# Where the weight sums for the last down projection are made: from the first layer's feed-forward part to the second layer's mixer

## The chip, the cores and the metric

The kernel runs on one core of a Trainium2 chip. The metric is device time in microseconds, the median of several runs. The engines are called by their names in the profile: PE is TensorE, PEld its weight loads, DVE is VectorE, ACT is ScalarE, POOL is GpSimd and SP is SyncE, which here only issues transfers.

## What is computed

A trunk of two layers over 512 tokens of width 1024, in float32. Each layer has three parallel mixers (a state recurrence, a chunked retention, a gated spatial unit), whose outputs are projected, gated and added, then an output projection and a feed-forward part with a short convolution. A root-mean-square norm stands before each half and at the end. Cut to what matters:

```
for l in range(2):
    h = rmsnorm(x, norm1_g[l])
    p = h @ w_in[l]
    y_rw, y_ret, y_sg = recurrence(p), retention(p), gating(p)
    proj = einsum('bsgc,gcd->bsgd', stack([y_rw, y_ret, y_sg]), w_branch[l])
    x = x + sum(sigmoid(gates(p)) * proj) @ w_out[l]
    x = x + conv_ffn(rmsnorm(x, norm2_g[l]), ffn_w_up[l], conv_w[l], conv_b[l], ffn_w_down[l])
return rmsnorm(x, final_g)
```

## The kernel before

Matrix products run in a float32 form that rounds its operands, so every operand is split in two: `hi` is the rounded value (a cast on ACT, line 139 for weights), `lo` what is left (a subtraction on DVE, line 140). A product is then three matmuls (line 156). Weights come in units of 128 rows by 512: SP loads a unit into a buffer called `wr` (line 126), ACT and DVE split it into `wh`/`wl` or `sh`/`sl`, and PE uses it for 12 matmuls of 128 x 512 in most stages. The order of the units is known from a first pass of the program (`plan`). A number by stage (`AHEAD`, 3 in the merges) says how many units ahead of the use a unit is split; three buffers `wr` (`NRAW`) let SP load ahead of that.

Products collect in PSUM: four accumulators `acc` and four tiles `sm`. In SBUF lie shared pools of tiles of 128 x 512 float32: `u` (`NU`, 31 tiles), `r` (16) and, outside the recurrence, `f` (39).

A scheduler orders the instructions on each engine: program order is priority, and what is not ready by its model of time may be passed by what is. On the chip each engine and each queue then runs its list in order. `keep_in_program_order` (written `po`) lets an instruction go only after the instruction traced just before it on its engine; what is traced later may still go ahead of it.

A layer's mixer begins with the projection and preparation of the recurrence (`rwkv`, `solve`), then its eight chunks. In a chunk PE's small matmuls (line 664) alternate with a copy `xb` on DVE (line 687), a copy `U` on ACT (line 701) and the state update on DVE (lines 712 and 713). Between these links `fill` puts units of other projections (`fillers`: gates, retention, gating) on PE. For each pair of chunks the output is normed (lines 723 to 733), with a power on POOL (line 732). After the recurrence come the gating projection and the recurrence's output (`sgu_v`, `rwkv_out`), then a list of steps, `SEQ`: S, H, U and Y are retention and gating steps, and 0, 2 and 1 are merges of the three branches, eight of each. A merge is one unit on PE, the gate loaded back by POOL (line 1034) and a product with it on DVE (line 1037); the sum over branches is made on POOL for branch 2 and on DVE for branch 1 (line 1040). From the 18th step on, `SEQ` has only merges. `wout` is the output projection: eight results of two units each, the residual sum (line 1051), the norm's operands (line 215) and squares (line 222).

The last down projection of the second layer is done as a fast product of halves with seven instead of eight products. For it four combinations of each group of four 128 x 512 tiles of the weight `wdt` are needed. They don't depend on the input, but the kernel makes them: `presum` loads four tiles `pre` on POOL's queue (line 253), makes four additions and subtractions on DVE in place (lines 242 to 245) and stores the results to HBM on POOL's queue (line 248). There are 11 such groups. They are made in the first layer: four in the up projections, with 16 tiles of the pool `f`, seven in the down projection, with tiles of the pool `u`. `last` reads the results as units named `tsum` (`ts` in the profile).

Of the kernel before, what the change touches and what calls it, by code (L numbers as in the profile page):

```python
# [15 lines left out]
L = 2  # L16
# [6 lines left out]
NU, NR, NFP = 31, 16, 39  # L23
FILL = (36, 2, 1)
KEPT = 6
PRE = {(0, "f", 2): 0, (0, "f", 4): 1, (0, "f", 6): 2, (0, "f", 8): 3, (0, "d", 0): 4, (0, "d", 1): 5, (0, "d", 2): 6, (0, "d", 3): 7,
       (0, "d", 4): 8, (0, "d", 5): 9, (0, "d", 6): 10}
SEQ = "0 H 0 S 0 U S U S 0 S 0 0 S 2 2 Y 0 0 2 1 2 1 2 1 2 1 2 1 2 1 1 1"
NRAW = 3
AHEAD = {None: 2, "p": 4, "r": 3, "f": 3, "u": 5, "q": 4}  # L30
# [21 lines left out]
class Emit:  # L52
    def __init__(self, ctx, tc, a, plan=None):

        self.plan, self.used = plan, []
        self.raws, self.parts, self.nraw, self.npart = [], [], 0, 0
        self.pool, self.fp, self.pin, self.keep, self.turn = None, None, False, False, 4
        self.tc, self.nc, self.a = tc, tc.nc, a
        tp = lambda n, b, **k: ctx.enter_context(tc.tile_pool(name=n, bufs=b, **k))
        self.cp = tp("cp", 1)  # L60
        self.wp = tp("wp", 2)
        self.up = tp("up", NU)
        self.rg = tp("rg", NR)
# [57 lines left out]
    def load(self, u):  # L121
        name, l, i, c0, n, _ = u
        raw = self.u(n="wr") if u[5] == "q" and self.nraw % 2 else self.wp.tile([128, 512], F32, name=self.nm("wr"), tag="wr", bufs=NRAW)
        src = self.tsum[i] if name == "tsum" else self.a[name][l, i]
# [112 lines left out]
    def presum(self, l, stage, m):  # L237

        if self.pre:
            q, b = self.pre.pop()  # L240
            V = self.nc.vector
            V.tensor_tensor(b[3], b[3], b[1], op=SUB)
            V.tensor_tensor(b[1], b[1], b[0], op=SUB)
            V.tensor_tensor(b[0], b[0], b[3], op=ADD)
            V.tensor_tensor(b[2], b[2], b[0], op=SUB)
            for p, t in zip((7, 5, 6, 4), (b[3], b[1], b[0], b[2])):
                self.tsum[q, p] = self.dp.tile([128, 512], F32, name=self.nm("ts"))
                self.nc.gpsimd.dma_start(self.tsum[q, p], t)
        q = PRE.get((l, stage, m))
        if q is not None:  # L250
            b = self.fpre.pop(0) if stage == "f" else [self.u(n="pre") for _ in range(4)]
            for i, t in enumerate(b):
                self.nc.gpsimd.dma_start(t, self.a["wdt"][0, 2 * q + i // 2][:, i % 2 * 512:i % 2 * 512 + 512])
            self.pre.append((q, b))
# [69 lines left out]
    def run(self):  # L324
        nc, tc, a, V = self.nc, self.tc, self.a, self.nc.vector
        self.con = self.cp.tile([128, NCC], F32, name="con")
        self.pre, self.tsum = [], {}
# [52 lines left out]
    def mixer(self, l, nst):  # L380
        self.pool = None
        with self.tc.tile_pool(name=f"rw{l}", bufs=1) as rp:
            self.rwp = rp
            self.filler = self.fillers(l)
# [18 lines left out]
        for step in (sg, sg, out, sg, None, out, sg, out, out):  # L403
            next(step) if step else self.sgu_bias()
        yrw, ysg, mg, out, m2 = self.yrw, [], [], [], 0
# [3 lines left out]
        for step in SEQ.split():  # L409
# [51 lines left out]
    def rwkv(self, l, nst):  # L461
# [211 lines left out]
        for c in range(8):  # L673
# [13 lines left out]
            V.tensor_copy(xb, Q[:, 1])  # L687
            self.fill(FILL[2], True)
# [12 lines left out]
            A.copy(U, P1[:, 1])  # L701
            self.fill(FILL[2], True)
# [4 lines left out]
            if c < 7:  # L707
# [3 lines left out]
                else:  # L711
                    V.tensor_tensor(St, St, Q[:, 0], op=ADD)
                    po(V.tensor_tensor(St, St, f, op=MUL))
            py = P1[:, 0]
# [328 lines left out]
    def wout(self, l, mg, xd, st):  # L1043
        nc, V = self.nc, self.nc.vector
        out = []
        for m in range(8):
# [6 lines left out]
            self.norm_z(st, xi, "n2")  # L1053
            self.norm_sq(st, xi)
# [3 lines left out]
    def ffn_up(self, l, st, x):  # L1058
# [58 lines left out]
    def ffn_down(self, l, act, x, st):  # L1117
# [3 lines left out]
        for m in range(8):  # L1121
# [8 lines left out]
            self.presum(l, "d", m)  # L1130
# [3 lines left out]
    def last(self, act):  # L1134
# [8 lines left out]
        def unit(p, q):  # L1143
            if p > 3:
                return self.unit("tsum", 0, (q, p), 0)
# [290 lines left out]
```

## Time and profile before

| | us |
|---|---|
| median of 3 runs | 1705.17 (1704.99 to 1705.78) |
| the profiled execution's own time | 1701.58 |
| its span, first to last instruction | 1699.7 |
| PE busy | 1687.0 |
| PEld busy | 1379.7 |
| DVE busy | 1233.1 |
| ACT busy | 799.9 |
| POOL busy | 240.8 |

The granted clock is 0.999 over the span. A busy time counts an engine's instructions from start to end; matmuls are pipelined, so PE counts as busy even where a matmul starts a little later than it could. The chain of waits follows the last instruction back to what released it, step by step. A row of a group names the line, the engine, the operation, what it writes and reads, and the count. Times along the span are in microseconds from its start.

### The profile page before, as it was taken

The numbers are of one execution on the slowest core, as the hardware profiler recorded it, in microseconds if no ns is written. First come the engines' busy times: TensorE is split into PE (matmuls) and PEld (weight loads), VectorE is DVE, ScalarE is ACT, GpSimd is POOL, SyncE is SP. The second block draws the span as 40 slices with busy tenths as digits, with TensorE's granted clock in tenths as the row PEclk, the third lists the DMA queues.
The fourth block names the chain that finished last, engine by engine and source line by source line (L and its number), as shares of the span: only waits on it lengthen the run. The fifth ranks groups of instructions, "written<-read, shape, count | busy, mean of one in ns | idle before, by whom it ended". The sixth has DMA issues, their size and how long they took to land.

```text
span 1699.7 us, 27885 instructions
## 1 busy us (share of the span) xinstructions
PE 1687.0 (99%) x10214; PEld 1379.7 (81%) x10214; DVE 1233.1 (73%) x2157; ACT 799.9 (47%) x1367; POOL 240.8 (14%) x336
## 2 busy tenths in 40 slices
PE   9999999999999999999999999999999999999998
PEld 7888777888888888888888888777888888887786
DVE  6887746578669887655568888455775698888776
ACT  6563433554355444433355644335542554444565
POOL 2121000003301200003321210000132022110000
PEclk9999999999999999999999999999999999999999
DMA  5236552524544532147743365525254443433774
GB/s 182 87 108 203 177 179 94 181 92 161 189 146 147 194 123 95 63 145 260 255 142 100 97 211 172 180 94 188 85 173 149 155 136 132 130 131 112 241 243 167
DMA packets 147768, 260.01 MB, mean 153 GB/s; under 512 B 19600, under 2 KB 39952, under 8 KB 147632
## 3 DMA queue, kind: packets, MB, share of 16 engines
q1 hardware_dynamic: 122960, 192.87, 35.2%
q0 software_dynamic: 15888, 49.95, 8.7%
q10 hardware_dynamic: 8784, 15.42, 2.6%
q8 instruction: 80, 1.31, 0.3%
q14 instruction: 56, 0.46, 0.1%
HBM read 212.94 MB, written 45.22 MB: 152 GB/s over the span
## 4 chain that ended last, share of the span: by engine, by line
PE 90%; DVE 4%; DMA 3%; issue 1%; ACT 1%; SPq 0%; ACTq 0%; DVEq 0%
PE acc L156 82%; PE sm L156 3%; PE sm L664 2%; DVE wl L140 1%; DMA wr<-wall 1%; PE sm L917 1%; PE sm L571 1%; DMA tr<-bkT 1%; DVE sl L140 0%; PE sm L1022 0%; ACT wh L139 0%; DVE cs L790 0%; DMA wr<-ts 0%; DVE TMP L788 0%; DMA x<-xT 0%
## 5 line engine op out<-in xcount | busy, mean ns | idle before, releaser
L156 PE MATMUL acc<-lo,sh 128*128 128x512 f32 x1108 | 431.8, 390 | 0.5 <-ACT sh L139 0.5
L156 PE MATMUL acc<-hi,sh 128*128 128x512 f32 x1108 | 431.9, 390 | 0.0
L156 PE MATMUL acc<-hi,sl 128*128 128x512 f32 x1108 | 430.3, 390 | 0.2 <-DVE sl L140 0.2
L139 ACT CAST sh<-wr 128x512 fp32r<-128x512 f32 (+1 forms) x375 | 228.3, 615 | 370.3 <-PE acc L156 217.6
L140 DVE TENSOR_TENSOR sl<-wr,sh 128x512 fp32r<-128x512 f32 (+1 forms) x375 | 254.5, 684 | 103.5 <-ACT sh L139 78.3
L140 DVE TENSOR_TENSOR wl<-wr,wh 128x512 fp32r<-128x512 f32 x238 | 166.5, 703 | 144.5 <-ACT wh L139 141.1
L139 ACT CAST wh<-wr 128x512 fp32r<-128x512 f32 x238 | 146.8, 619 | 244.4 <-PE acc L156 160.3
L156 PEld LDWEIGHTS acc<-lo,sh 128*128 128x128 f32 x1108 | 208.0, 188 | 45.0 <-ACT sh L139 1.2
L156 PEld LDWEIGHTS acc<-hi,sl 128*128 128x128 f32 x1108 | 208.0, 188 | 44.1 <-DVE sl L140 0.7
L156 PEld LDWEIGHTS acc<-hi,sh 128*128 128x128 f32 x1108 | 208.0, 188 | 43.1 <-issue 0.3
L156 PE MATMUL acc<-lo,wh 128*128 128x512 f32 x588 | 232.3, 395 | 0.3 <-DVE lo L215 0.2
L156 PE MATMUL acc<-hi,wl 128*128 128x512 f32 x588 | 229.8, 391 | 0.5 <-DVE wl L140 0.5
L156 PE MATMUL acc<-hi,wh 128*128 128x512 f32 x588 | 229.3, 390 | 0.0
L156 PEld LDWEIGHTS acc<-lo,wh 128*128 128x128 f32 x588 | 110.5, 188 | 25.5 <-DVE lo L215 1.5
L156 PEld LDWEIGHTS acc<-hi,wl 128*128 128x128 f32 x588 | 110.4, 188 | 25.4 <-DVE wl L140 1.5
L156 PEld LDWEIGHTS acc<-hi,wh 128*128 128x128 f32 x588 | 110.6, 188 | 22.5 <-issue 0.2
L156 PE MATMUL acc<-ah,sh 128*128 128x512 f32 x352 | 108.4, 389 | 0.0
L1084 ACT ACTIVATE cv<-fu,pc 128x512 f32<-128x512 f32 x88 | 71.6, 816 | 61.1 <-DVE fu L1082 59.8
L1082 DVE TENSOR_TENSOR fu<-acc,rsF 128x512 f32<-128x512 f32 x88 | 60.6, 688 | 39.8 <-PE acc L156 39.7
L156 PE MATMUL acc<-wl,hi 128*128 128x512 f32 x212 | 86.1, 406 | 0.0
L156 PE MATMUL acc<-wh,lo 128*128 128x512 f32 x212 | 82.8, 391 | 0.0
L156 PE MATMUL acc<-wh,hi 128*128 128x512 f32 x212 | 82.7, 390 | 0.0
(359 smaller groups left out, 2426.8 us busy)
## 6 DMA issues: line engine op xcount, KB each, us to landing
wr<-wall SPq DMA_DIRECT2D x488, 256.0 KB, 2.8
gd<-gth ACTq DMA_DIRECT2D x48, 256.0 KB, 3.0
gth<-gd POOLq DMA_DIRECT2D x48, 256.0 KB, 3.5
pre<-wdt POOLq DMA_DIRECT2D x44, 256.0 KB, 5.9
ts<-pre POOLq DMA_DIRECT2D x44, 256.0 KB, 2.8
wr<-ts SPq DMA_DIRECT2D x44, 256.0 KB, 3.9
wr<-wdn SPq DMA_DIRECT2D x40, 256.0 KB, 4.2
wr<-wdt SPq DMA_DIRECT2D x33, 256.0 KB, 3.6
```

The source lines that it names most:

```text
L139: self.kept(self.nc.scalar.copy(hi[:, :n], raw[:, :n]))
L140: self.kept(self.nc.vector.tensor_tensor(lo[:, :n], raw[:, :n], hi[:, :n], op=SUB))
L156: i = self.nc.tensor.matmul(*x, **y, **kw)
L571: i = T.matmul(pK[hv[1 - h], j, :], bk[hv[h], c, 1, :], x[hv[h], c, :], start=True, stop=True)
L664: po(T.matmul(o, l, r, start=start, stop=True, skip_group_check=True))
L917: po(T.matmul(X[h][:, i, :], lhsT, rhs, start=new[h], stop=stop, skip_group_check=True))
L1082: V.tensor_tensor(u, ps, self.rsF, op=MUL)
L1084: A.activation(t, u, AF.Identity, scale=self.p("cw2", j), bias=self.p("cb", j))
```

## The change

The groups of four sums are made in the second layer instead. A generator `sums` does it in steps: four loads on POOL; an empty step; then each operation on DVE, followed one step later by its store on POOL; each is kept behind what was traced before it on its engine. `presum` advances the generator: three times in each chunk of the second recurrence (after the copy `xb`, after the copy `U`, after the state update), once for each of the nine steps after it, twice for each of the 16 late steps of `SEQ`, and in the output projection five times for the first result and twice for each other. In the first layer the generator is empty. Four tiles of an own pool `pp` hold the loads. The pool `u` grows from 31 to 33 tiles, and the area for the descriptors of POOL's transfers is set to 4096 bytes a partition; the 16 tiles of `f` and the tiles of `u` are no longer taken for the sums.

```diff
-NU, NR, NFP = 31, 16, 39
+NU, NR, NFP = 33, 16, 39
-PRE = {(0, "f", 2): 0, (0, "f", 4): 1, (0, "f", 6): 2, (0, "f", 8): 3, (0, "d", 0): 4, (0, "d", 1): 5, (0, "d", 2): 6, (0, "d", 3): 7,
-       (0, "d", 4): 8, (0, "d", 5): 9, (0, "d", 6): 10}
+RING = 4096
...
+        self.pp = tp("pp", 4)
...
-    def presum(self, l, stage, m):
-
-        if self.pre:
-            q, b = self.pre.pop()
-            V = self.nc.vector
-            V.tensor_tensor(b[3], b[3], b[1], op=SUB)
-            V.tensor_tensor(b[1], b[1], b[0], op=SUB)
-            V.tensor_tensor(b[0], b[0], b[3], op=ADD)
-            V.tensor_tensor(b[2], b[2], b[0], op=SUB)
-            for p, t in zip((7, 5, 6, 4), (b[3], b[1], b[0], b[2])):
-                self.tsum[q, p] = self.dp.tile([128, 512], F32, name=self.nm("ts"))
-                self.nc.gpsimd.dma_start(self.tsum[q, p], t)
-        q = PRE.get((l, stage, m))
-        if q is not None:
-            b = self.fpre.pop(0) if stage == "f" else [self.u(n="pre") for _ in range(4)]
+    def sums(self, l):
+
+        P, V, po = self.nc.gpsimd, self.nc.vector, self.tc.keep_in_program_order
+        for q in range(NFF // 2 if l else 0):
+            b = [self.pp.tile([128, 512], F32, name=self.nm("pre"), tag="pre") for _ in range(4)]
             for i, t in enumerate(b):
-                self.nc.gpsimd.dma_start(t, self.a["wdt"][0, 2 * q + i // 2][:, i % 2 * 512:i % 2 * 512 + 512])
-            self.pre.append((q, b))
+                po(P.dma_start(t, self.a["wdt"][l - 1, 2 * q + i // 2][:, i % 2 * 512:i % 2 * 512 + 512]))
+            yield
+            yield
+            for p, o, x, op in ((7, 3, 1, SUB), (5, 1, 0, SUB), (6, 0, 3, ADD), (4, 2, 0, SUB)):
+                po(V.tensor_tensor(b[o], b[o], b[x], op=op))
+                yield
+                self.tsum[l, q, p] = self.dp.tile([128, 512], F32, name=self.nm("ts"))
+                po(P.dma_start(self.tsum[l, q, p], b[o]))
+            yield
+
+    def presum(self, n=1):
+        for _ in range(n):
+            next(self.sum, None)
...
-            self.filler = self.fillers(l)
+            self.filler, self.sum = self.fillers(l), self.sums(l)
...
         for step in (sg, sg, out, sg, None, out, sg, out, out):
             next(step) if step else self.sgu_bias()
+            self.presum()
...
-        for step in SEQ.split():
+        for i, step in enumerate(SEQ.split()):
+            self.presum(2 if i > 16 else 0)
...
             V.tensor_copy(xb, Q[:, 1])
+            self.presum()
             self.fill(FILL[2], True)
...
             A.copy(U, P1[:, 1])
+            self.presum()
             self.fill(FILL[2], True)
...
                     po(V.tensor_tensor(St, St, f, op=MUL))
+            self.presum()
...
             self.norm_z(st, xi, "n2")
+            self.presum(2 if m else 5)
             self.norm_sq(st, xi)
...
-        if l == 0:
-            self.fpre = [[self.f(n="pre") for _ in range(4)] for _ in range(4)]
         for i in range(NFF):
-            if l == 0 and i % 2 == 0 and 2 <= i <= 10:
-                self.presum(l, "f", i)
...
             xd.append(d)
-            self.presum(l, "d", m)
...
-        nc = _bacc.Bacc("TRN2", target_bir_lowering=False, num_devices=1)
+        nc = _bacc.Bacc("TRN2", target_bir_lowering=False, num_devices=1, dynamic_dma_scratch_size=RING)
```

More of the change, by code (lines that the diff above doesn't have):

```diff
@@ L123, in load @@
         raw = self.u(n="wr") if u[5] == "q" and self.nraw % 2 else self.wp.tile([128, 512], F32, name=self.nm("wr"), tag="wr", bufs=NRAW)
-        src = self.tsum[i] if name == "tsum" else self.a[name][l, i]
+        src = self.tsum[(l, *i)] if name == "tsum" else self.a[name][l, i]
         with self.tc.high_priority():
@@ L326, in run @@
         self.con = self.cp.tile([128, NCC], F32, name="con")
-        self.pre, self.tsum = [], {}
+        self.tsum = {}
         self.rst = self.cp.tile([128, 512], F32, name="rst")
@@ L1144, in unit @@
             if p > 3:
-                return self.unit("tsum", 0, (q, p), 0)
+                return self.unit("tsum", L - 1, (q, p), 0)
             return self.unit("wdt", 0, 2 * q + (p > 1), 512 * (p == 3))
```

## The prediction

> **What bounds the kernel now.** I read the busy times first, then the chain of waits, then the busy times by stage, then the waits around the sums.
>
> ```profile
> span 1699.7 us, 27885 instructions
> PE 1687.0 (99%) x10214; PEld 1379.7 (81%) x10214; DVE 1233.1 (73%) x2157; ACT 799.9 (47%) x1367; POOL 240.8 (14%) x336
> PE 90%; DVE 4%; DMA 3%; issue 1%; ACT 1%; SPq 0%; ACTq 0%; DVEq 0%
> ```
>
> TensorE is busy for nearly the whole span and makes 90% of the chain that ended last. Whether it runs at its pace is read from the long pieces of the chain:
>
> ```profile
> 509.76 355.19 PE acc L156 x1567
> ...
> 1262.79 94.05 PE acc L156 x414
> ...
> 1357.30 210.36 PE acc L156 x928
> ```
>
> 355.19 / 1567 = 0.2267 us for each matmul, the same in the second layer (210.36 / 928 = 0.2267), and 0.2272 in the stretch of the second layer's merges and output projection. The granted clock is 1.00 in these stages (next table), so a unit of 12 such matmuls takes 2.72 us and no stage runs below it. Only matmuls that start late can be won or lost.
>
> The busy times by stage (columns: window, its length, PE, PEld, DVE, ACT and POOL busy with counts, granted clock, DMA share, GB/s). The rows are: the first layer's output projection and feed-forward part, the second layer's recurrence, its gating projection, its early merges, its late merges, its output projection, and the passage into the last product.
>
> ```profile
> 460.00:860.00 400.00, 400.00 (x1766) 331.34 (x1765) 285.25 (x449) 170.11 (x274) 49.38 (x92) 1.00 0.48 161
> 1060.00:1142.00 82.00, 81.78 (x1180) 63.32 (x1178) 42.22 (x86) 30.46 (x59) 7.15 (x7) 1.00 0.44 141
> 1142.00:1208.00 66.00, 65.29 (x319) 53.25 (x315) 39.30 (x73) 35.27 (x64) 3.58 (x4) 1.00 0.45 144
> 1208.00:1265.00 57.00, 57.00 (x342) 47.58 (x341) 46.30 (x95) 26.23 (x51) 15.23 (x19) 1.00 0.44 148
> 1265.00:1309.00 44.00, 44.00 (x195) 36.24 (x194) 30.61 (x46) 13.81 (x23) 13.94 (x18) 1.00 0.50 162
> 1309.00:1347.00 38.00, 38.00 (x170) 31.45 (x169) 23.95 (x38) 17.98 (x30) 0.00 (x0) 1.00 0.47 151
> 1550.00:1600.00 50.00, 48.67 (x209) 38.57 (x208) 39.58 (x66) 22.80 (x38) 4.32 (x8) 1.00 0.49 152
> ```
>
> In 460 to 860, where the sums are made now, TensorE is busy 400.00 of 400 us with 1766 matmuls; 400 / 0.2267 = 1764, so not one is missing. The late merges are as full: 195 matmuls, 44 / 0.2267 = 194. Where time is lost, windows of 50 us show it (PE busy with its count):
>
> ```profile
> 1150.00:1200.00 50.00, 49.29 (x217) 1.00 0.55 178
> 1300.00:1350.00 50.00, 50.00 (x222) 1.00 0.46 148
> 1550.00:1600.00 50.00, 48.67 (x209) 1.00 0.49 152
> 1550.00:1600.00 50.00, 48.67 (x209) 1.00 0.49 152
> ```
>
> A full window has 222. The row of 1150 lacks 5 (1.1 us), that of 1550 lacks 13 (2.9 us).
>
> **What is taken out.** 44 subtractions and additions, 44 loads and 44 stores leave the first layer's feed-forward part. By the first row above this wins nothing, though VectorE is freed: no matmul there started late. I take 0; the bounds are 0.5 us to either side, the two matmuls by which the counts differ. What hides the work now is TensorE's full queue; the tiles that it held are freed for the same stage and win nothing either.
>
> **What is put in.** All of it goes to the second layer, in 77 steps of the generator, seven to a sum of four (loads, nothing, first operation, then three times store and operation, then the last store). The recurrence calls it 24 times, the projection after it 9, the late merges 32, the output projection up to 19. That places 13 operations in the recurrence, 6 in the projection, 17 in the late merges and 8 in the output projection. The durations:
>
> ```profile
> L253 POOL DMA_DIRECT2D pre<-wdt x44: 536/538/543, 455.8 to 845.6; - x44
> L248 POOL DMA_DIRECT2D ts<-pre x44: 539/543/548, 538.7 to 856.7; - x44
> L242 DVE TENSOR_TENSOR pre<-pre,pre x11: 685/691/695, 537.7 to 853.6; 128x512 f32<-128x512 f32 x11
> pre<-wdt POOLq DMA_DIRECT2D x44, 256.0 KB, 5.9
> ts<-pre POOLq DMA_DIRECT2D x44, 256.0 KB, 2.8
> ```
>
> One operation takes 0.69 us alone. In a queue the next one starts sooner, as one instance in the first layer's down projection shows:
>
> ```profile
> 755.40 2.14 POOL L253 DMA_DIRECT2D pre<-wdt  x4
> ```
> ```profile
> 763.99 0.69 DVE L242 TENSOR_TENSOR pre<-pre,pre 128x512 f32<-128x512 f32 x1 [3.20 <-DMA pre<-wdt]
> ...
> 766.05 0.69 DVE L140 TENSOR_TENSOR sl<-wr,sh 128x512 fp32r<-128x512 f32 x1
> 766.65 0.69 DVE L245 TENSOR_TENSOR pre<-pre,pre 128x512 f32<-128x512 f32 x1
> 767.26 1.28 DVE L140 TENSOR_TENSOR sl<-wr,sh 128x512 fp32r<-128x512 f32 x2
> ```
>
> From 766.05 to 766.65 to 767.26 is 0.60 us each, so an added operation costs VectorE 0.60 us. The same instance shows the wait that comes with it: four loads are issued from 755.40, the first operation starts 8.6 us later, and VectorE stood for 3.20 us until the last load had landed. Over that stage:
>
> ```profile
> DVE pre L242 <- DMA pre<-wdt: 15.8, 6, 3.3
> ```
>
> Six waits, 2.6 us in the mean, 3.3 at the longest. Such a wait holds all that is queued behind it on VectorE.
>
> **Recurrence (1060 to 1142).** VectorE is busy 42.22 of 82 us; 13 operations add 7.8. Each stands behind the copy of `xb`, the copy of `U` or the state update; behind it wait the casts of weights (`wl`), the filler's gating product and the next link of the chain, for which TensorE waits. The cover is the 12 filler matmuls between two links. It is thin at one place:
>
> ```profile
> 1124.92 0.41 DVE L712 TENSOR_TENSOR S<-S,sm 128x256 f32<-128x256 f32 x1
> ...
> 1126.18 0.42 DVE L713 TENSOR_TENSOR S<-S,F 128x256 f32<-128x256 f32 x1
> ```
> ```profile
> 1126.74 0.69 PE L664 MATMUL sm<-S,X 64*64 64x64 f32 x32 [0.22 <-DVE s L724]
> ...
> 1137.95 0.69 PE L664 MATMUL sm<-S,X 64*64 64x64 f32 x32
> ```
>
> At chunk 5 the state is ready at 1126.60 and TensorE waited 0.22 us for VectorE, because the rotations are in front; at chunk 6 the matmuls came without a wait, but close behind. One added operation in front of either costs up to 0.60 us: bounds 0 and 1.2, and I take 0.6. Nothing is removed here, so there is no gain. POOL's power of the norm and the two tables' loads stand behind a load or a store of 0.54 us each, and behind the operation that a store waits for; what they give is read a whole filler later. SP issues none of the added transfers.
>
> **Gating projection (1142 to 1208).** 6 operations, 3.6 us, into 27 us of idle VectorE. TensorE loses 1.1 us here already; it could go or double, so the bounds are -1.1 and 1.1, and I take 0.2, since work is added and none taken.
>
> **Late merges (1265 to 1309).** Here the sum is decided. VectorE is busy 30.61 of 44 us, so 13.4 are free. 17 operations take 17 x 0.60 = 10.2; 3.2 are left. POOL, busy 13.94, gets 20 loads and 18 stores, 38 x 0.54 = 20.5: 34.5 of 44, enough, but in order. A store waits for its operation and a load for a free buffer, and behind them on POOL wait the gates' loads and the additions, for which VectorE's last merges wait. Between a group's loads and its first operation lies one merge (2.72 us) by the order of calls, against the 8.6 us of the instance. The scheduler can put other work in between, as it did there, so I take its wait, 2.6 us, for each of four groups: 10.4. The transfers say much the same from their side: the stage moves 162 GB/s, 7.1 MB; 38 transfers add 10.0 MB; at 283 / 0.85 = 333 GB/s, by the row of 1600 above, 44 us move 14.7 MB, so 2.4 MB or 7.4 us come late. (The weights of SP share this; by the code they are fetched three units and more ahead.) VectorE then owes 10.2 + 10.4 - 13.4 = 7.2 us at the end of the stage. POOL's additions are in the way as well:
>
> ```profile
> 1300.98 1.15 DVE L140 TENSOR_TENSOR sl<-wr,sh 128x512 fp32r<-128x512 f32 x1 [0.78 <-ACT sh L139]
> ```
> ```profile
> 1300.29 1.29 POOL L1040 TENSOR_TENSOR gth<-gth,gth 128x512 f32<-128x512 f32 x1 [3.77 <-DVE gth L1037]
> ```
>
> The cast beside POOL's addition took 1.15 instead of 0.69 us. There are six such additions here, 6 x 1.29 = 7.7 of 44 us, so 3 of 17 operations meet one: 1.4 us, in all 8.6. [...]
>
> The cover: weights are cast ahead of use, and there are four accumulators, so a merge's product on VectorE may be late by up to 3 units, 8.2 us, before TensorE lacks one. It is late by up to one unit already:
>
> ```profile
> 1266.18 1.28 DVE L1037 SCALAR_TENSOR_TENSOR gth<-gth,acc 128x512 f32<-128x512 f32 x2
> ```
>
> Two merges' products run back to back, 2.72 us of TensorE's work apart. So 5.5 to 8.2 us are covered, and of 8.6 between 0.4 and 3.1 come through. The longest wait (3.3) for each group would add 2.8; no wait at all leaves no debt. Bounds 0 and 5.9; a gain is excluded, as no matmul is missing. I take 1.8, the middle of what the mean wait gives. What is late next is the last merged tile, and with it the output projection.
>
> [...]
>
> **Output projection (1309 to 1347).** 8 operations (4.8 us) and two waits (5.2) into 14 us of idle time: I take 0, bounds 0 and 2.7, a unit's worth. Behind a wait stand the residual sums (`xi`) and the norm's squares; if that cover is gone, the first up projection is late.
>
> **Passage into the last product.** The two further shared tiles can let weights be loaded and cast sooner there:
>
> ```profile
> 1571.61 1.89 DVE L140 TENSOR_TENSOR sl<-wr,sh 128x512 fp32r<-128x512 f32 x3
> ```
> ```profile
> 1576.25 2.81 DMA wr<-ts
> ...
> 1581.65 2.73 DMA wr<-ts
> ```
>
> The chain runs over three casts in a row and over loads of the finished sums, and 2.9 us are lost. Most of it is VectorE's own work, which tiles don't shorten, and nothing is added here. Bounds -2.9 and 0; I take -0.4. The smaller descriptor area could make POOL wait for room: the 88 issues above take 536 to 548 ns, so none waited, and by the calls no more than eight transfers are open. If each had to wait for the one before (2.8 us), 38 would take 106 of 44 us; I take 0.
>
> **Sum.** 0 + 0.6 + 0.2 + 1.8 + 0 - 0.4 = 2.2 us. The profiled execution took 1701.58 us (span 1699.7 and 1.9 around it), 3.6 below the median of the runs, 1705.17. With the same distance 1703.8 becomes 1707.4 us. That is within 0.2% (3.4 us), about the least that a measurement of this kernel can tell from no change.
>
> **Rivals.** *The groups' own loop becomes the bound of the late merges (slower).* With four buffers a group can't begin before the last store of the one before has landed: store 2.8 us, load 5.9, and the issues, 9 us; with four operations over one and a half merges (4.1) it is 13.1, where the calls allow 3.5 merges, 9.5. If VectorE stands behind each, four groups are 4 x 3.6 = 14.4 us late, of which 8.2 are covered: 6.2, and with the other terms' 0.4 the time is 1711.8 us. It decides, that is passes 0.2%, from about 3.2 us of wait a group (10.2 + 1.4 + 12.8 - 13.4 - 8.2 = 2.8, and 0.4). For it: 3.3 was measured, and the transfers there will be denser. Against it: the scheduler laid the waits of the first layer too, and TensorE lost nothing by them.
>
> *The two tiles close the passage (faster).* The 2.9 us there and the 1.1 at 1150 go, the added stages cost nothing: -4.0, 1701.2 us. Against it: VectorE is busy 39.58 of 50 there.
>
> *The sums don't stay where they are put.* Unpinned on one side, they drift past the merges, where they find room in the output projection and the up projections: 0.6 + 0.2 - 0.4, 1705.6 us. For it: an operation is pinned only behind what was traced before it.
>
> **How the numbers follow.** Forecast 0.37 and drift 0.16 both lie within 0.2%; the loop 0.36 and the descriptor area 0.04, slower; the closed passage 0.07, faster. So 0.07, 0.53, 0.40. The time is that of the forecast. The range goes from 1702.3, the passage at its bound of -2.9 and nothing added, to 1714.5, the loop with the smaller cover of 5.5 (8.9 + 0.4): 7% lie below, 12% above.
>
> **What would show it.** The first layer's stretch has the same count of matmuls for each 50 us and less VectorE work. In the late merges VectorE is busy near 41 of 44 us, waits of 2 to 3 us for `pre` loads stand before the sums, and TensorE has gaps of 2 us in all. The loop shows such waits over 3.2 us and TensorE waiting for the merges' products or tiles between 1265 and 1320; the drift shows `pre` operations in the up projections. I am wrong in kind if TensorE loses time at a place where no sum runs, or if the first layer gets shorter.

## The result: 1.2% slower, and the profile after

| | before | after |
|---|---|---|
| median, us | 1705.08 (1703.74 to 1705.78) | 1725.72 (1724.16 to 1726.11) |
| ratio of the times | | 1.012, 95% interval 1.0103 to 1.0138 |
| the profiled execution's own time | 1701.58 | 1724.16 |
| its span | 1699.7 | 1722.5 |

The forecast was 1707.4 us and the top of its range 1714.5. Both are too low; the sign was held as the less likely one. The busy times and the engines' shares of the chain don't show what happened. In the new kernel's page:

```profile
span 1722.5 us, 27812 instructions
PE 1692.8 (98%) x10214; PEld 1381.6 (80%) x10214; DVE 1235.5 (72%) x2157; ACT 799.1 (46%) x1367; POOL 243.7 (14%) x336
```

VectorE and POOL are as busy as before (1233.1 and 240.8), since the same work has only moved. The busy times by stage of the kernel after show the loss (columns as in the prediction). The rows are the first layer's feed-forward part, the recurrence, the late merges and the output projection:

```profile
460.00:860.00 400.00, 400.00 (x1767) 331.31 (x1766) 259.84 (x406) 169.79 (x271) 3.79 (x7) 1.00 0.34 105
1050.00:1150.00 100.00, 95.99 (x1385) 74.67 (x1384) 58.99 (x116) 39.17 (x78) 21.66 (x31) 1.00 0.65 210
1271.00:1335.00 64.00, 55.22 (x231) 43.90 (x230) 46.03 (x67) 15.41 (x25) 32.03 (x51) 0.95 0.75 258
1335.00:1373.00 38.00, 34.98 (x154) 28.30 (x153) 27.04 (x44) 16.49 (x28) 8.12 (x15) 1.00 0.78 262
```

The same windows of the kernel before:

```profile
1050.00:1150.00 100.00, 99.78 (x1416) 77.76 (x1415) 51.08 (x102) 41.23 (x81) 7.15 (x7) 1.00 0.44 141
1271.00:1335.00 64.00, 64.00 (x284) 52.77 (x283) 39.95 (x61) 22.99 (x39) 12.61 (x17) 1.00 0.49 161
1335.00:1373.00 38.00, 38.00 (x169) 31.46 (x168) 29.87 (x46) 21.12 (x32) 3.68 (x7) 1.00 0.40 125
```

The first layer is untouched: 1767 matmuls in 400 us, 1766 before. In the recurrence TensorE stood for 99.78 - 95.99 = 3.8 us more. In the late merges 284 - 231 = 53 matmuls of 0.2267 us are missing, 12.0 us. In the output projection 15 are missing, 3.4 us. That makes 19.2 of the 22.8 us by which the span grew; the rest lies in single late matmuls before 500 us (2.6, where profiles of the kernels below differ by up to 5) and in the passage into the last product (0.9). (By the medians the loss is 20.6 us; the profiled execution of before was 3.5 us below its median, that of after 1.6.) So more than half of the loss is in the late merges, for which the forecast had 1.8.

Whom TensorE waited for, in the kernel after (us in total, times, longest):

```profile
PE acc L156 <- DVE gth L1043: 8.3, 4, 5.4
PE acc L156 <- DVE xi L1057: 3.0, 2, 1.6
PE sm L667 <- DVE S L718: 2.4, 3, 1.3
```

These are the merges' products, the residual sums of the output projection and the recurrence's state. VectorE itself waited for the sums' loads (`DVE pre L247 <- DMA pre<-wdt`) only 4.4 us in three waits, one of them of 2.9 us in the recurrence. So the prediction's waits of 2.6 us at each group did not come. What held the product at the longest gap is read from POOL's timeline (start, duration, instruction, in brackets the idle time before it):

```profile
1285.92 1.50 POOL L1046 TENSOR_TENSOR gth<-gth,gth 128x512 f32<-128x512 f32 x1
1287.37 0.56 POOL L250 DMA_DIRECT2D ts<-pre  x1
1288.88 0.54 POOL L250 DMA_DIRECT2D ts<-pre  x1 [0.96 <-DVE pre L247]
1289.41 1.07 POOL L243 DMA_DIRECT2D pre<-wdt  x2
1290.47 1.06 POOL L1040 DMA_DIRECT2D gth<-gd  x2
```

and from the chain of waits of the same kernel after it:

```profile
1290.47 5.50 DMA gth<-gd
1296.00 0.70 DVE gth L1043
1296.84 4.58 PE acc L156 x11
```

The next two gates were issued 4.55 us after the addition (1285.92 to 1290.47), behind two stores and two loads of the sums, and landed 5.5 us later; TensorE started at 1296.84 after a gap of 5.76 us. Of that, VectorE stood 3.34 us for these gates. In the whole stretch from 1230 to 1400 it stood for gates no more than

```profile
DVE gth L1043 <- DMA gth<-gd: 4.3, 3, 3.3
```

so late gates are a part of the merges' 12.0 us and not the whole. In the kernel before nothing stood between (POOL's timeline):

```profile
1275.11 1.29 POOL L1040 TENSOR_TENSOR gth<-gth,gth 128x512 f32<-128x512 f32 x1 [3.11 <-DVE gth L1037]
1276.35 1.09 POOL L1034 DMA_DIRECT2D gth<-gd  x2
1280.60 1.29 POOL L1040 TENSOR_TENSOR gth<-gth,gth 128x512 f32<-128x512 f32 x1 [3.16 <-DVE gth L1037]
```

This is a loop: addition, gates' load, product, addition. Before, one round took 5.49 us, and two merges take TensorE 2 x 2.72 = 5.44. The load issued at 1276.35 landed after 3.0 to 3.5 us and the product started at 1279.83, 3.48 us after the issue. That a round is as long as two merges doesn't show by itself that the loop is full, since TensorE sets the same pace. The six additions of the stretch are 5.44, 5.49, 8.16, 5.44 and 6.09 us apart, and VectorE waited for no gate; its waits from 1265 to 1310 were these:

```profile
DVE sl L140 <- ACT sh L139: 10.4, 11, 1.4
DVE lo L149 <- ACT hi L148: 2.7, 4, 0.7
```

The loop's own steps tell more: 1.24 us from the addition to the issue, 3.1 us (the median of the stretch) to the landing, 0.77 us from the product's start to the next addition. That is 5.1 us, an estimate from these rows, and it leaves 0.3 us of the 5.44, less than one issue of 0.54. Beyond that only the accumulators are a reserve.

### The profile page after: what moved, and what is told of

Read it like the earlier page. It is cut to its first block, busy times and chain, and to the rows that moved or that the text cites. A ratio compares the mean times of both kernels' runs of the same rounds, so it can differ in the third digit from the quotient of the medians.

```text
span 1722.5 us, 27812 instructions
## 1 busy us (share of the span) xinstructions
PE 1692.8 (98%) x10214; PEld 1381.6 (80%) x10214; DVE 1235.5 (72%) x2157; ACT 799.1 (46%) x1367; POOL 243.7 (14%) x336
## 4 chain that ended last, share of the span: by engine, by line
PE 78%; DMA 8%; issue 6%; DVE 5%; ACT 2%; POOL 1%; SPq 0%; ACTq 0%; POOLq 0%; DVEq 0%
PE acc L156 71%; DMA wr<-wall 3%; PE sm L156 2%; PE sm L667 2%; DVE wl L140 1%; DMA pre<-wdt 1%; PE sm L923 1%; DMA gth<-gd 1%; DVE sl L140 1%; PE sm L574 1%; DMA tr<-bkT 1%; DMA wr<-wdt 1%; ACT wh L139 1%; ACT sh L139 0%; PE sm L1028 0%
```

## The experiments

Four theories were put to the test. *VectorE*: the 44 operations stand in front of products and casts. *Traffic*: the sums' bytes make the gates, weights and residuals land late. *Queue* (later *loop* or *POOL*): what the sums put on POOL's queue holds the gates' loads. *Order* (added for e13 to e15): the order that the scheduler lays down for VectorE changed. Medians in us, the ratio to the kernel before on the same chip in the same session, and PE's matmuls in the window 1271 to 1335 (284 before):

| run | us | ratio, 95% interval | matmuls |
|---|---|---|---|
| the change | 1725.72 | 1.0120 (1.0103 to 1.0138) | 231 |
| e1_pools | 1704.3 | 1.0001 (0.9992 to 1.0011) | 284 |
| e2_first_layer | 1702.85 | 0.9995 (0.9985 to 1.0004) | 283 |
| e3_not_late | 1707.87 | 1.0026 (1.0015 to 1.0038) | 284 |
| e4_gates_sp | 1725.17 | 1.0131 (1.0107 to 1.0155) | 234 |
| e5_small_transfers | 1717.51 | 1.0077 (1.0055 to 1.0098) | 228 |
| e6_small_ops | 1725.82 | 1.0121 (1.0093 to 1.0148) | 224 |
| e7_both_small | 1716.53 | 1.0072 (1.0052 to 1.0092) | 227 |
| e8_half_merges | 1716.91 | 1.0079 (1.0050 to 1.0109) | 245 |
| e9_bare_issues | 1715.24 | 1.0065 (1.0050 to 1.0080) | 239 |
| e10_more_f | 1722.22 | 1.0107 (1.0091 to 1.0122) | 215 |
| e11_gates_act | 1726.95 | 1.0138 (1.0120 to 1.0156) | 237 |
| e12_late_stores | 1723.96 | 1.0127 (1.0110 to 1.0144) | 219 |
| e13_order_kept | 1733.89 | 1.0171 (1.0138 to 1.0204) | 189 |
| e14_issues_order_kept | 1712.18 | 1.0045 (1.0030 to 1.0060) | 256 |
| e15_small_transfers_order_kept | 1721.82 | 1.0095 (1.0066 to 1.0125) | 213 |
| e16_first_more_f | 1701.65 | 0.9983 (0.9966 to 0.9999) | 283 |
| e17_sums_sp | 1741.07 | 1.0218 (1.0201 to 1.0235) | 198 |
| e18_small_transfers_sp | 1718.67 | 1.0084 (1.0069 to 1.0099) | 248 |

Line numbers above 140 differ by a few between these kernels.

**Which part costs.** The pools and the descriptor area alone, on the kernel before:

```diff
-NU, NR, NFP = 31, 16, 39
+NU, NR, NFP = 33, 16, 39
+RING = 4096
```

> The kernel before with only the pools of the change: 33 shared tiles and a descriptor area of 4096 bytes; the sums stay in the first layer. Queue theory (the gates' loads stand behind and among the sums' transfers on POOL's queue): 1705, within 2 us. VectorE theory (the sums' operations and their waits hold the merges' products): 1705 as well. Pool theory (the smaller descriptor area or the other tiles cost the time): 1715 to 1726.

Then the changed kernel with its generator stepped in the first layer only:

```diff
-        for q in range(NFF // 2 if l else 0):
+        for q in range(NFF // 2 if l == 0 else 0):
...
         for i in range(NFF):
+            if l == 0:
+                self.presum(4)
```

> The changed kernel with the same generator, four tiles, pools and descriptor area, but stepped four times in each pass of the first layer's up projections instead of in the second layer. No gates are loaded there and VectorE has room. Queue theory and VectorE theory: 1704 to 1707. Pool theory, or a cost of four tiles as such: 1715 to 1726.

And the changed kernel without the steps in the late merges and the output projection:

```diff
-            self.presum(2 if i > 16 else 0)
...
-            self.presum(2 if m else 5)
...
+            if l:
+                self.presum(4)
```

> The changed kernel without steps in the late merges and the output projection; the 44 steps left over run in the second layer's up projections, four in a pass. Queue theory: the loss of the late merges and the output projection goes (about 11.5 and 3.6 us), that of the recurrence (4 us) stays: 1709 to 1712. VectorE theory: the same there, but the up projections, where VectorE is fuller, lose some: 1711 to 1716. Pool theory: 1725.

Pools, area, generator and the four own tiles cost nothing that can be measured. The place is what costs: some 16 us in the late merges and the output projection together, 4.5 in the recurrence and the gating projection. The 44 remaining steps of e3, dense as they are, cost nothing in the second layer's up projections.

**Bytes or operations.** The sums' transfers cut to an eighth (e5), the operations cut to an eighth (e6), both (e7):

```diff
-                po(P.dma_start(t, self.a["wdt"][l - 1, 2 * q + i // 2][:, i % 2 * 512:i % 2 * 512 + 512]))
+                po(P.dma_start(t[:, :64], self.a["wdt"][l - 1, 2 * q + i // 2][:, i % 2 * 512:i % 2 * 512 + 64]))
...
-                po(P.dma_start(self.tsum[l, q, p], b[o]))
+                po(P.dma_start(self.tsum[l, q, p][:, :64], b[o][:, :64]))
```
```diff
-                po(V.tensor_tensor(b[o], b[o], b[x], op=op))
+                po(V.tensor_tensor(b[o][:, :64], b[o][:, :64], b[x][:, :64], op=op))
```

> The changed kernel with 64 of the 512 columns in each of the sums' 44 loads and 44 stores (four lasting tiles, zeroed once; the last product loads other blocks of the same size in place of the sums; so part of the sums is left out). All 44 operations, all issues and their order on POOL's queue stay. Traffic theory (the sums' bytes fill the DMA engines to 0.75 in the merges, so gates, weights and residuals land late): most of the 21 us goes, 1705 to 1711 us. VectorE theory (44 operations in front of the products and casts) and queue theory (gates' loads stand on POOL's queue behind stores that wait for an operation): 1718 to 1726 us, as those are all still there.

> The changed kernel with the 44 operations on 64 of 512 columns each (so the sums are left unfinished); loads, stores, issues and their order stay. VectorE theory: most of the 21 us goes, 1706 to 1712 us. Traffic theory: 1719 to 1726 us. Queue theory: the waits of the stores for their operation get some tenths of a us shorter each, 1715 to 1723 us.

> Both cut to 64 columns (so the sums are left unfinished): what is left is 88 issues on POOL of 0.54 us, in their order and with their waits, and 44 very short operations on VectorE. Queue theory: still 1712 us or more. Traffic and VectorE theory, alone or together: 1703 to 1708 us. If this one is fast and each of the two others slow, both resources must be given way at once.

The VectorE theory fell: its operations took 0.22 instead of 0.69 us and the time stayed (1725.82). Small transfers took away 8.2 us (7.3 by the ratios), and cutting the operations as well added nothing to that that can be told (1716.53). With 1717.51 us e5 lies between the answers that the theories gave. But the 8.2 us did not come from the merges, where the traffic theory looked first. The windows of e5:

```profile
1050.00:1150.00 100.00, 98.98 (x1400) 77.29 (x1399) 60.46 (x118) 40.63 (x80) 21.86 (x31) 1.00 0.49 153
1271.00:1335.00 64.00, 55.93 (x228) 44.38 (x227) 45.05 (x63) 14.87 (x25) 32.27 (x52) 0.95 0.44 136
1335.00:1373.00 38.00, 38.00 (x169) 31.46 (x168) 30.55 (x49) 19.73 (x33) 8.41 (x16) 1.00 0.54 172
```

The recurrence got 3.0 of its 3.8 us back (2.1 in e7, which has the same transfers) and the output projection all 3.4, so the bytes cost there. The late merges lost 228 against 284 matmuls, 12.7 us, at a DMA share of 0.44, lower than before the change. Where the bytes cost in the recurrence, the chain of the kernel after shows:

```profile
1096.69 5.33 DMA pre<-wdt
...
1102.64 5.02 DMA wr<-wall
...
1108.41 0.69 DVE wl L140
...
1110.03 0.69 PE sm L667 x32
```

A group's load lands after 5.3 us, VectorE stands for it, the next weight is called late and takes 5.0 us for the 3.0 in the median of that stretch before, its cast stands in front of the state update, and the chain's next link waits. In the output projection the `xi` loads stand on SP behind such weights: VectorE waited five times for them, 5.9 us (three times before, 2.7 us).

**How much of it, and what of it.** Half the density in the merges (e8: one step a merge, the rest in the up projections), and then nothing but issues (e9): each load and store a copy of 64 columns within DRAM that needs no tile and no operation, and no operations at all:

```diff
-            b = [self.pp.tile([128, 512], F32, name=self.nm("pre"), tag="pre") for _ in range(4)]
+            b = [self.dp.tile([128, 64], F32, name=self.nm("pre")) for _ in range(4)]
...
-                po(V.tensor_tensor(b[o], b[o], b[x], op=op))
...
-                po(P.dma_start(self.tsum[l, q, p], b[o]))
+                po(P.dma_start(self.tsum[l, q, p], self.a["wdt"][l - 1, 2 * q][:, o * 64:o * 64 + 64]))
```

> The changed kernel with one step instead of two at each late merge, none in the output projection, and the rest in the second layer's up projections, four at a pass: half the sums' work in the late merges. The recurrence's and the gating projection's 4.5 us stay. Traffic theory: 7.1 MB of the kernel before and 5 MB of sums lie below what the DMA engines can move in the 44 us, so the merges add 0 to 2: 1708 to 1711 us. Queue theory: half as many held gates' loads, half the 12 us: 1713 to 1716 us. VectorE theory: 5 us of operations into 13 us free, 1708 us.

> The changed kernel in which each of the 44 loads and 44 stores is a copy of 64 columns within DRAM that waits for nothing, without the 44 operations (so the sums are left out; the last product loads other blocks of the same size in their place). What is left of the change is 88 issues of 0.54 us on POOL's queue at their places. If POOL's time alone holds the gates, the late merges lose most of their 12 us as before: 1712 us or more. If it is the waits of the issues (a store for its operation, a load for a freed tile), that stand in front of the gates' loads: 1703 to 1708 us.

Half the steps cost 284 - 245 = 39 matmuls, 8.8 us, in the merges: less than the whole, more than half. The bare issues still lost 45 matmuls, 10.2 us. So neither the sums' bytes nor their operations nor their waits are needed for the late merges' loss: the issues on POOL are enough. How they cost there is not by late gates (VectorE waited 2.0 us for them), as the chain of e9 shows:

```profile
1276.48 8.25 PE acc L156 x35
...
1284.80 0.63 ACT sh L139
...
1285.45 0.69 DVE sl L140
1286.14 0.61 DVE gth L1042
...
1286.79 10.97 PE acc L156 x47
```

TensorE ends a unit, which frees a tile for the next weight's cast on ScalarE and VectorE; behind that cast on VectorE stands a product that has long been possible, and for its accumulator TensorE waits 2.1 us. There are four such gaps. The order of casts (c) and products (g) on VectorE from 1271 us, read from the two timelines:

```
before  ccggccgcgccggccgcgcgcgcgcg
e9      ccgggcccgggcgcccggcgcgccggcgcgc
```

Before, never more than two casts stand between products; here twice three. Two of the four gaps stand behind these; the other two stand behind two casts, with products kept back. In e1, e2, e3 and e16, which have no steps in the merges, the order of casts and products is that of before; in every kernel that has steps there and no tie of order (below), three or four casts stand between products at some place. So the order of casts and products changes with the added steps, even where these are bare issues.

**Where the loads stand.** The gates issued by SP (e4) or ScalarE (e11); two more tiles for the merges (e10); each store one step later, so that it seldom waits (e12):

```diff
-        nc.gpsimd.dma_start(t, self.gd[br, m])
+        (nc.sync if l else nc.gpsimd).dma_start(t, self.gd[br, m])
```
```diff
-NU, NR, NFP = 33, 16, 39
+NU, NR, NFP = 31, 16, 41
```

> The changed kernel with the second layer's gates loaded on SP's queue instead of POOL's; all else stays. Queue theory: the gates no longer stand behind the sums, and 6 to 11 us of the late merges' loss go: 1714 to 1720. VectorE theory: no change, 1724 to 1727, as its operations and waits stay. Traffic theory (the sums' transfers slow the gates' by the shared transfer engines alone): no change either, 1723 to 1727.

> The changed kernel with the second layer's gates loaded by ScalarE's queue instead of POOL's. Loop theory: the loads no longer stand behind the sums' issues and waits: 1712 to 1718 us, if ScalarE's casts of weights, now behind a gate's load that waits for its tile, have room. If the gates' place on a queue is not what costs, or ScalarE is held as SP was: 1722 us or more.

> The changed kernel with two more tiles in the pool of the merges (NFP 41 for 39) and two fewer in the pool of weights (NU 31 for 33). Loop theory: in the late merges a pair of gates is loaded into the tiles that POOL's addition has just freed, about 3 us before it is used, and all that the sums put on POOL comes between; two more tiles give two merges (5.4 us) more, and most of the merges' 12 us goes: 1711 to 1717 us. If tiles are not what the gates' loads wait for: 1721 to 1727 us.

> The changed kernel with each store issued one step later than its operation (the last two together), so that POOL does not wait for an operation that has just been queued; everything else as in the changed kernel. If the stores' waits for VectorE's operations hold the gates' loads: 1714 to 1720 us. If it is POOL's time or the loads' waits for freed tiles (a tile is now freed later): 1723 to 1728 us.

None of the four helped by more than 3.5 us. e4 came out where the queue theory didn't have it, but it doesn't settle whether POOL's queue is the cause. SP's timeline has the gates behind weights there, which wait for their tiles,

```profile
1280.91 5.57 SPq L126 DMA_DIRECT2D wr<-wall  x2
1286.57 0.88 SPq L1040 DMA_DIRECT2D gth<-gd  x2
```

so the gates moved from one queue on which they waited to another (VectorE waited ten times for them between 1230 and 1400, 13.7 us; with ScalarE's queue eleven times, 14.0). Tiles were not what the loads lacked (e10), nor were the stores' waits what held them (e12).

**Order or loop.** One tie: a weight's cast stands on VectorE behind the last merge's product traced before it, so that the two alternate. On the whole change (e13), on the bare issues (e14), on the small transfers (e15):

```diff
+            if pool == "r" and u[1] and len(self.prods) > 32:
+                self.tc.add_manual_dep(i.ins, self.prods[-1].ins.name, mybir.DependencyInfo(mybir.DependencyClass.NoSync, mybir.DependencyReason.DATA), reason="order")
```

> The whole change, with one tie of order added: in the late merges a weight's cast on VectorE stands behind the last merge's product that is traced before it, so that casts and products alternate, as in most of the kernel before, and never three casts stand in front of two products. Order theory: the 12 us of the late merges shrink to what the late gates cost by traffic (0 to 4); the recurrence's 4 and the output projection's 3.6 stay: 1710 to 1716 us. POOL theory (its issues and waits hold the gates' loads): 1721 to 1727 us.

> The 88 bare issues on POOL (the sums are left out, as before), with the same tie of order. Order theory: the 11 us go, 1703 to 1707 us, though POOL issues as much as without the tie. POOL theory: 1712 us or more, as without it.

> The transfers cut to 64 columns (part of the sums is left out), all operations and waits there, with the same tie of order. If order (12 us) and traffic (8 us) are the whole: 1703 to 1708 us. If POOL's waits or VectorE's operations cost something of their own in the merges: 1709 us or more.

The order theory fell as a whole explanation. With bare issues the tie lowered the late merges' loss from 10.2 to 28 matmuls, 6.3 us (by the times 3.1 us, with intervals that overlap). What was left shows late gates, as the chain of e14 has them:

```profile
1290.24 0.21 POOL gth L1049
...
1291.85 0.53 POOL ts L253
1292.38 4.94 DMA gth<-gd
...
1297.41 0.70 DVE gth L1046
...
1298.19 1.67 POOL gth L1049
...
1300.35 2.06 POOL pre L247 x4
1302.41 2.98 DMA gth<-gd
...
1305.48 0.70 DVE gth L1046
...
1306.26 1.23 POOL gth L1049
```

From addition to addition 7.95 and 8.07 us, for two merges of 5.44. The first round is long by a landing of 4.94 us behind a single issue, the second by five issues, 2.6 us, before a landing of 2.98. With the order kept, VectorE waited 12.9 us for gates in the stretch from 1230 to 1400, where it was 2.0 in e9. (The recurrence of e14 stood 99.78 - 97.09 = 2.7 us longer than before, that of e9 did not; no run shows why.) On the whole change the tie made it worse (1733.89): a cast now stands behind a product that waits for a late gate (19.1 us in six waits), and TensorE waits for the casts as well (4.6 us). With small transfers it was the same in kind: 1721.82 with the tie, 1717.51 without, with intervals that overlap.

**The sums off POOL.** Last, the sums' transfers issued by SP, with all bytes (e17) and with small ones (e18):

```diff
-        P, V, po = self.nc.gpsimd, self.nc.vector, self.tc.keep_in_program_order
+        P, V, po = self.nc.sync, self.nc.vector, self.tc.keep_in_program_order
```

> The whole change, but the sums' 44 loads and 44 stores are issued by SP instead of POOL, so that between POOL's addition and the next gates' loads nothing of the sums is left. Loop theory: the merges' 12 us go but for what traffic costs there (the gates' loads land 1 to 2 us later); the recurrence's and the output projection's losses by traffic stay or grow, as weights now stand behind stores on SP: 1708 to 1716 us. If the loop over POOL is not the cause: 1721 us or more.

> The same with 64 of 512 columns in each of the sums' transfers (part of the sums is left out; the last product loads other blocks of the same size). All 44 operations stay on VectorE, all 88 issues stand on SP. If the loop over POOL (10 to 12 us) and the traffic (8 us) are the whole: 1703 to 1707 us, against 1717.5 with the same transfers on POOL. If VectorE's operations or the waits for them cost something of their own: 1709 us or more.

Both came out against the loop theory: e17 in the range that was to show that the loop over POOL is not the cause, e18 in the one that leaves a cost to VectorE's operations or their waits. In e18 the gates were on time (VectorE waited 0.5 us for them), and the late merges still lost 36 matmuls, 8.2 us; the recurrence lost 99.78 - 94.50 = 5.3. In e17, with all bytes, the late merges lost 86, 19.5 us, and its chain there runs through the sums:

```profile
1303.20 3.60 PE acc L156 x8
1306.80 6.48 DMA ts<-pre
...
1313.29 2.48 DMA pre<-wdt
...
1315.80 0.70 DVE pre L247
```

A store, the load into its tile and the operation behind it hold VectorE's next product. On SP weights now stand behind the sums' stores (1302.27 and 1302.87 in e18), as gates did on POOL. So the late merges lose time with none of the sums' issues on POOL as well, and with the gates on time. What costs in e18 is not told apart: its 44 operations, which cost nothing with the issues on POOL (e6, e7), the waits around them, or the order, which has three casts between products here too.

**A version ahead of both.** e2 with the two pools of e10, the sums in the first layer:

> The sums made by the changed kernel's generator in the first layer's up projections, where they cost nothing, with NFP 41 for 39 and NU 31 for 33: with these pools the passage into the last product lost 1.6 us in its trace for 3.6 before. If that was the pools: 1701 to 1702 us, 0.1 to 0.2% faster than before. If it was chance of the run: 1703 to 1705 us.

Its ratio, 0.9983, lies just below 1 with its whole interval. Between 1550 and 1600 us, where the kernel before had 209 matmuls, its profile has 219, and that of e2, which differs by the pools alone, 209:

```profile
1550.00:1600.00 50.00, 49.81 (x219) 40.60 (x217) 41.46 (x71) 24.04 (x39) 5.39 (x10) 1.00 0.44 139
```

It is the only version here that beats the kernel before, by 0.17% and barely clear of noise, and the change's move is not in it. Its profiled execution, 1706.1 us, was among its slowest, with 19 matmuls fewer than before in the first 500 us, so the gain of the median can't be followed through its trace.

## Why the prediction was wrong

**Right**: the stretch of the first layer wins nothing (400.00 of 400 us, as forecast); pools and the smaller descriptor area cost nothing (e1); the costs lie in the second layer, and most in the late merges; the gating projection lost nothing (between 1150 and 1271 TensorE stood for 0.34 us, 0.71 before).

**Late merges, forecast 1.8 us (bounds 0 and 5.9), measured 12.0.** The step that failed is the sum of VectorE's debt, 10.2 for operations and 10.4 for waits against 13.4 free. It failed in mechanism, not in size alone. With operations of 0.22 us the loss was no smaller (e6), and of the waits for group loads, put at 4 x 2.6, the merges had 1.5 us. The sentence beside it named the right place and priced it at nothing: POOL's 34.5 of 44 us were "enough, but in order". In its place the runs showed that the issues alone, without the sums' bytes, operations and waits, cost 10.2 us there (e9). Busy time was the wrong measure. Two ways are seen by which issues cost. One is POOL's place in the loop from addition to gates' load to product: at the longest gap of the changed kernel four issues and a wait stood between the addition and the gates (4.55 us instead of 1.24), and e14 has rounds of 8 us. The rows for this stood in the trace of before; the prediction read POOL's additions there as neighbours that make an operation beside them longer (1.15 us for 0.69 in its instance), and not as the start of the next loads. The other is the order on VectorE: in e9 the gates were nearly on time (2.0 us of waits). The term of 1.4 us for sums that meet POOL's additions did not come on the sums: all 44 took 0.67 to 0.70 us. It came on two casts of 1.19 and 1.79 us (starts 1286.78 and 1318.47), each of which ended 0.55 us after the addition, as the prediction's instance did (1302.13 against 1301.58).

The same section's cover of 5.5 to 8.2 us by four accumulators was assumed to be free. Part of it was in use: before, five rounds of the loop took 30.6 us for ten merges of 2.72, so the products fell back by 3.4 us. In e9 they come in twos and threes behind two or three casts, and four times TensorE stood for an accumulator. That the list of *other* instructions would be written anew was a step that the prediction lacks. It spoke of the scheduler as one that may put other work in between, or let the sums drift.

**Recurrence, forecast 0.6 (bounds 0 and 1.2), measured 3.8.** The prediction costed 13 operations and left out the wait for a group's load, which it put at 2.6 us in the merges; here one came, of 2.9. The bytes cost (3.0 of 3.8 came back in e5, 2.1 in e7), by a late weight's cast in front of the state update. "SP issues none of the added transfers" is true and misled: the DMA share went from 0.44 to 0.65, and a weight that SP issued landed after 3.8 us in the median instead of 3.0 (3.0 again in e5, with an eighth of the sums' bytes).

**Output projection, forecast 0 (bounds 0 and 2.7), measured 3.4.** The place was named, behind a wait stand the residual sums; but it was the residual's own load that was late, by traffic (all came back in e5). The estimate that 2.4 MB or 7.4 us of transfers come late is near the 8.2 us that the bytes cost in all, but by luck: it was made for the late merges, where small transfers won nothing (228 matmuls for 231). It was set aside as "much the same from their side", a second reading of VectorE's debt; the bytes were a cost of their own, in other stages. The rate of 333 GB/s in it goes by a row that the prediction's list doesn't show (it has the row of 1550 twice). The trace of before has it:

```profile
1600.00:1650.00 50.00, 50.00 (x222) 1.00 0.85 283
```

**Passage, forecast -0.4.** Nothing came of it (e1: 1.0001); the pools of e10 and e16 do shorten it, by another division of the same tiles.

**Rivals.** The loop that I named was the groups' own, store to load through four tiles; the four waits of 3.2 us or more on `pre` that it needs are not there. The loop seen at the longest gap was another, the gates'. The drift did not come: the last operation of the sums starts at 1363.0, in the output projection.

**What stays open.** That issues on POOL suffice for some 10 of the late merges' 12 us is shown (e9). That they are needed is not: with the sums' issues on SP and small transfers 8.2 us were lost (e18). How much is the longer loop and how much the changed order is open too: the tie took away 3 to 4 of the 10 us with bare issues and cost 8 on the whole change, and the tie on the kernel before, without any sums, was not run. Also, the six POOL additions of the late merges took 1.65 to 1.67 us each in e14, where all six took 1.29 before, and the tie, which puts other VectorE work beside them, may be why. No run freed the late merges while all the sums' work was in them.

## What to carry to other kernels

Before work is put on a queue, look for the loops that run through it (a load whose issue follows an addition, whose product feeds the next addition) and add up the steps of one round. Here they came to 5.1 of the 5.44 us that TensorE needs for the same work, so there was less room than one issue of 0.54 us, though POOL was busy for only 13.94 of 44 us. The length of a round can't tell this, because the bound engine paces it. Added work showed up here in three ways that a busy table doesn't show: place on a queue, bytes that delay others' transfers, and another order of everything around it. To tell them apart, cut bytes, operations and waits one at a time with the issues left in place; moving the work to another queue only shows what is urgent there.

## What was not expected of the hardware

After the gap of 5.76 us TensorE's matmuls started 0.43 us apart, at half the pace, before they returned to 0.23; the granted clock of the late merges' window is 0.95. PE's timeline in the kernel after, around the gap:

```profile
1290.85 0.39 PE L156 MATMUL acc<-hi,sh 128*128 128x512 f32 x1
1291.08 0.39 PE L156 MATMUL acc<-hi,sl 128*128 128x512 f32 x1
1296.84 0.77 PE L156 MATMUL acc<-lo,sh 128*128 128x512 f32 x1 [5.37 <-DVE gth L1043]
...
1297.83 0.63 PE L156 MATMUL acc<-hi,sl 128*128 128x512 f32 x1
1298.25 0.63 PE L156 MATMUL acc<-lo,sh 128*128 128x512 f32 x1
```

Nine starts are late by about 0.2 us each, 1.9 us on top of the gap. The length of a gap alone doesn't decide it here (gaps from start to start): in e9 one of four gaps of 2.2 to 2.3 us was followed by seven matmuls at half pace (41 matmuls took 11.11 us behind it, 47 took 10.97 behind another), and in e4 a gap of 3.8 us by none (24 matmuls took 5.92 us behind it). So in e9 a stall of 2.1 us cost 3.8, and what decides whether the pace falls is not shown.

The loads of 256 KB on POOL's queue for the sums took 4.9 us in the median in the kernel after (5.9 before, in the first layer), and the gates, of the same size, 3.1 in the late merges before and 4.8 after. With 32 KB (e5) a load of the sums took 2.5.
